# Weight slots of 16 KB: a decoder layer whose weights are laid out so that a partition's part of one load is one row of memory

## The chip, the core and the metric

The kernel runs on one NeuronCore of a Trainium2 chip. The metric is the device time of one execution in microseconds; the median of three runs is shown for the kernel before. The profile is that of one execution, taken by the hardware profiler. Its engines are PE (matmul; PEld is its weight load), DVE (vector), ACT (scalar), POOL (GpSimd) and SP (here it only issues DMAs). The data moves on 16 DMA engines.

## The reference

One post-norm decoder layer on 256 tokens of width 1024, all float32. First attention with 8 heads: with a sequence of 256 and blocks of 256 there is no earlier block to select, so it is causal softmax attention over the 256 tokens with a relative-position bias. Then a mixture of 32 experts of which each token takes 4:

```python
qkv = (x @ w_in).reshape(B, S, 3, H, Dh)
s_own = q @ k^T * scale + rel_t[:, t5_bucket(rel_own)]      # causal
t = softmax(s_own) @ v @ w_out
h = layer_norm(ALPHA * x + t, ln_g[0], ln_b[0])
logits = h @ w_router + b_router                            # top 4 of 32, softmax over the 4
for each expert e, on its tokens:
    g, u = split(h @ w_gu[e] + b_gu[e])                     # 1024 x 2048
    a = min(g, 7) * sigmoid(1.702 * min(g, 7)) * (clip(u, -7, 7) + 1)
    y += gate * (a @ w_dn[e] + b_dn[e])                     # 1024 x 1024
out = layer_norm(ALPHA * h + y, ln_g[1], ln_b[1])
```

The expert weights are 32 x (8 + 4) MB, about 403 of the 426 MB that the kernel moves, and each is read once.

## The kernel before

The program is one straight sequence per engine, in the order in which the Python code calls the instructions (`manual_schedule`); semaphores are put in for what depends on what. SP issues nearly all DMAs, in order; an issue stands on SP until its target buffer is free and until the load eight issues earlier on the same semaphore has landed, and everything behind it on SP stands with it.

*Slots.* SBUF holds 24 slots of 8 KB a partition (128 x 2048 float32, 1 MB), all from one pool, `wp`. `slot` (L89) takes one; `drop` (L98) gives some back and calls `prefetch` (L128), which fetches as many further weight chunks as there are free slots above `reserve`. Weights come through these slots in a fixed order, the list `todo`: 12 half blocks of w_in (blocks in the order 0, 2, 1, 3, 4, 5), 4 chunks of w_out, then for each expert 8 chunks of w_gu (`("gu", e, k)`, 128 rows of 2048) and 4 of w_dn (`("dn", e, j)`, 2 x 128 rows of 1024). `source` (L101) says where in DRAM a chunk stands: for w_gu a partition's part is one row of 8 KB, for w_in one row of 8 KB (the host has put it so), for w_dn and w_out two rows of 4 KB that lie 512 KB apart.

*Attention* (to about 90 us). x and the weights are split into a float32r high part and a remainder (`split`, L139: a cast on ACT into `whi`, a subtraction on DVE into `wlo`), and a product is three float32r matmuls (L283 to L285 for q and k, L309 to L311 for v, L418 to L421 for the output projection). A split takes two further slots, and gives the chunk's own back when it is done. `rel_bias` (L234) sends a table through DRAM (`rd`) and reads it back as `BT`. Small tensors have slots of their own: xh, xl, BT (later x), QT (later the gain), V, KTt, xT, then h and hT, biases, first, acts, Ys, acc.

*Router and first gather* (to 128 us): the four best experts for each token, positions in each expert's 64 slots, one-hot matrices.

*Experts* (128 to 1060 us), two at a time. `stage1` (L599) puts the bias into PSUM (L603) and then, for k = 0 to 7, waits for chunk k, does four matmuls with it (L610) and gives its slot back (`after(k)`). Then come on DVE and ACT the activation, on PE the scatter of the earlier expert (L663), the gather for the next pair (L593) and transposes (L627, L649). `stage2` (L630) does the same with the four w_dn chunks, four matmuls each (L638). After the last expert come a loop for experts with more than 64 tokens (`more_blocks`, which does not run on these inputs: only its branch shows, L714), the last scatter (L837) and the second norm.

```python
for k in range(KT):
    w = chunk(k)
    for i in range(2):
        for s in range(2):
            q = 2 * i + s
            nc.tensor.matmul(hgu[i][s * 64:(s + 1) * 64], xg(k), w[:, q * 512:(q + 1) * 512], ...)
    after(k)
```

Of the kernel before, what the change touches and what calls it, by code (L numbers as in the profile page):

```python
# [23 lines left out]
NE, TOPK = 32, 4  # L24
# [10 lines left out]
W_SLOTS = 24  # L35
CONV = 3
# [25 lines left out]
def tile_decoder_layer(ctx: ExitStack, tc, a, out):  # L62
# [49 lines left out]
    todo = [("in", b, i) for b in ORDER for i in range(2)] + [("out", 0, j) for j in range(4)]  # L112
    for e in range(NE):
        todo += [("gu", e, k) for k in range(KT)] + [("dn", e, j) for j in range(4)]
# [3 lines left out]
    def fetch(pieces=1):  # L118
        key = todo.pop()
        src = source(key)  # L120
        t = slot("w")
        k = src.shape[1]
        for i in range(pieces):
            ks = slice(i * k // pieces, (i + 1) * k // pieces)
            nc.sync.dma_start(t.rearrange("p (k c) -> p k c", k=k)[:, ks], src[:, ks])
        w_tiles[key] = t

    def prefetch():  # L128
        while todo and free_slots() > reserve[0]:
            fetch(1 if len(todo) > 1 else 2)  # L130
# [7 lines left out]

    def split(key, hi_engine, pieces=2, between=None):  # L139
        """The chunk as two float32r tiles that add up to it exactly."""  # L140
        w = take(key)
        hi, lo = slot("whi", FR), slot("wlo", FR)
        n = 2048 // pieces
# [6 lines left out]
        w_tiles["hi", key], w_tiles["lo", key] = hi, lo  # L150
        done(key)

    def done_split(key):
        done(("hi", key))
        done(("lo", key))
# [7 lines left out]
    class Stats:  # L163
        """Mean and (variance + eps)^-0.5 of rows that come in halves."""
# [14 lines left out]
        def finish(self):  # L179
            """One Newton step on the root that ScalarE gave."""  # L180
# [17 lines left out]
    xh, xl = (slot(n, FR).rearrange("p (k s) -> p k s", k=KT) for n in ("xh", "xl"))  # L198
    BT, QT, V = (slot(n) for n in ("BT", "QT", "V"))
    x, gb1, V = (t.rearrange("p (t d) -> p t d", t=2) for t in (BT, QT, V))  # L200
    BT, QT, KTt = (t.rearrange("p (h s) -> p h s", h=H) for t in (BT, QT, slot("KTt")))
# [7 lines left out]
    xT = slot("xT")  # L209
    xT3 = xT.rearrange("p (k s) -> p k s", k=KT)  # L210
    key0 = todo.pop()
    w0 = slot("w")
    w_tiles[key0] = w0
    w03 = w0.rearrange("p (k c) -> p k c", k=4)
    X_PARTS = (slice(0, 1), slice(1, 4), slice(4, 8))
    for i in range(4):
        if i < 2:
            nc.sync.dma_start(xT3[:, X_PARTS[i]], a["xT"][:, X_PARTS[i]])
        nc.sync.dma_start(w03[:, i:i + 1], source(key0)[:, i:i + 1])
    nc.sync.dma_start(xT3[:, X_PARTS[2]], a["xT"][:, X_PARTS[2]])  # L220
    fetch(2)
    nc.sync.dma_start(rb, a["rel_bias"])
    nc.sync.dma_start(oh, a["onehot"])
    for _ in range(4):
        fetch()
# [8 lines left out]
    def rel_bias():  # L234
# [4 lines left out]
        fetch()  # L239
# [26 lines left out]
    def parts(key, k):  # L266
        return tuple(take((p, key)).rearrange("p (k c) -> p k c", k=k) for p in ("hi", "lo"))
# [98 lines left out]
    for n in range(12):  # L366
# [28 lines left out]
    reserve[0] = 3  # L395
    drop(2)
# [32 lines left out]
    def norm_T(t, matmuls=None):  # L429
        """The normal rows transposed, with gain and shift on the way out of PSUM."""  # L430
# [21 lines left out]
    for j in range(2):  # L452
# [6 lines left out]
        if j == 0:  # L459
            for p in ("hi", "lo"):  # L460
                w_tiles.pop((p, ("out", 0, j)))
            used[0] -= 2
            h, hT = slot("h").rearrange("p (t d) -> p t d", t=2), slot("hT").rearrange("p (k s) -> p k s", k=KT)
# [19 lines left out]
    used[0] -= 2  # L483
    biases, first = slot("biases"), slot("first")
# [6 lines left out]
    drop()  # L491
# [11 lines left out]
    def top_experts(t):  # L503
        """The four largest logits, the lower index first where two are equal, beside four columns that are larger."""
# [6 lines left out]
    def positions(t):  # L511
        """Which of its expert's slots each choice takes: the number of earlier tokens with that expert."""
# [50 lines left out]
    drop()  # L563
# [35 lines left out]
    def stage1(xg, chunk, onehot_e, after):  # L599
# [30 lines left out]
    def stage2(aT, chunk, swap, Y, after, apart=False):  # L630
        banks = [pm.tile([128, 512], F32, name=n) for n in (("yp", "hg") if apart else ("yp",))]
        y_ps = [banks[s * apart][s * 64:(s + 1) * 64] for s in range(2)]
        for j in range(4):
            w = chunk(j).rearrange("p (k c) -> p k c", k=2)
            for k in range(2):
                kk = 2 * j + k
# [287 lines left out]
```

## Time and profile before

| | us |
|---|---|
| median of 3 runs (1080.9 to 1082.19) | 1081.65 |
| profiled execution, first to last instruction | 1077.4 |
| PE busy | 1016.4 (94%) |
| DVE busy | 239.6 (22%) |
| ACT busy | 172.3 (16%) |
| DMA, GB/s over the span | 396 |

The profiled execution gives its span alone; the median of the runs lies 4.25 us above it, for what stands ahead of the first and behind the last instruction. Times in the rows below are microseconds from the span's start. PE's matmuls are pipelined and their ends are modelled, so the starts of instructions are better read than their busy time: a matmul row that stands late behind its predecessor was waiting. TensorE's granted clock is 1.00 of full speed in nearly all of the span.

### The profile page before, as it was taken

What the parts mean: (1) busy time and instruction counts of PE and PEld (TensorE: products, weight loads), DVE (VectorE), ACT (ScalarE), POOL (GpSimd) and SP (SyncE); (2) the same over time, 40 slices, a digit from 0 to 9 for tenths busy, and PEclk for the clock granted to TensorE, in tenths of its full rate; (3) what the DMA queues carried; (4) which work ended last, traced back from release to release, by engine and by line L of the source; (5) the groups of instructions that cost most, each with busy time, mean ns of one, the idle gap of its engine ahead of it and who ended that gap; (6) DMA issues with size and microseconds to landing.
All of it is one profiled execution on the core that took longest, in us unless ns stands there. A gap on an engine that the chain in (4) does not pass through costs nothing. (4 is left out here: it accounts for less than half of the span.)

```text
span 1077.4 us, 11967 instructions
## 1 busy us (share of the span) xinstructions
PE 1016.4 (94%) x4970; PEld 443.9 (41%) x4970; DVE 239.6 (22%) x495; ACT 172.3 (16%) x316; POOL 15.4 (1%) x17
## 2 busy tenths in 40 slices
PE   9999999999999999999999999999999999999994
PEld 8988743343434343433324242323224242323331
DVE  6575602111111111111111111111101111111114
ACT  5454311011101010111101010101001010101012
POOL 0000300000000000000000000000000000000001
PEclk9999899999999999999999999999999999999998
DMA  9997799999999999999999999999999999999992
GB/s 330 411 367 272 264 375 384 419 415 418 416 418 418 419 417 417 416 416 417 416 418 418 417 418 416 417 417 417 416 417 417 418 418 417 415 415 418 418 413 88
DMA packets 78248, 426.39 MB, mean 396 GB/s; under 512 B 6793, under 2 KB 8113, under 8 KB 44113
## 3 DMA queue, kind: packets, MB, share of 16 engines
q1 hardware_dynamic: 77632, 423.52, 96.9%
q0 software_dynamic: 560, 2.10, 0.6%
q8 instruction: 40, 0.66, 0.2%
q14 instruction: 16, 0.12, 0.0%
HBM read 424.53 MB, written 1.06 MB: 395 GB/s over the span
## 5 line engine op out<-in xcount | busy, mean ns | idle before, releaser
L610 PE MATMUL hg<-w,xg 128*64 128x512 f32 x960 | 251.2, 601 | 26.3 <-DMA w<-in_w_gu 26.2
L610 PE MATMUL hu<-w,xg 128*64 128x512 f32 x960 | 246.7, 592 | 0.0
L638 PE MATMUL yp<-w,acts 128*64 128x512 f32 x1008 | 228.1, 598 | 11.2 <-ACT acts L628 11.2
L617 DVE TENSOR_SCALAR acts<-hg 128x512 f32<-128x512 f32 x32 | 22.1, 692 | 746.2 <-PE hg L610 746.2
L610 PEld LDWEIGHTS hg<-w,xg 128*64 128x64 f32 x960 | 61.0, 136 | 187.8 <-issue 102.7
L638 PEld LDWEIGHTS yp<-w,acts 128*64 128x64 f32 x1008 | 70.8, 137 | 146.2 <-issue 124.9
L610 PEld LDWEIGHTS hu<-w,xg 128*64 128x64 f32 x960 | 69.0, 137 | 137.0 <-issue 137.0
L618 ACT ACTIVATE acts<-acts 128x512 f32<-128x512 f32 x32 | 20.1, 630 | 500.2 <-DVE acts L617 500.2
L642 ACT COPY Ys<-yp 64x512 f32<-64x512 f32 x63 | 36.5, 580 | 219.2 <-PE yp L638 212.2
L593 PEld LDWEIGHTS tp<-OH,h 128*128 128x128 f32 x480 | 56.9, 192 | 8.1 <-issue 6.7
L663 PE MATMUL o<-Ys,GT 128*128 128x512 f32 x120 | 59.5, 618 | 0.0
L593 PE MATMUL tp<-OH,h 128*128 128x128 f32 x480 | 59.3, 277 | 0.0
L147 DVE TENSOR_TENSOR wlo<-w,whi 128x1024 fp32r<-128x1024 f32 (+1 forms) x36 | 38.1, 1103 | 16.3 <-ACT whi L158 16.1
L658 DVE TENSOR_TENSOR acc<-o,acc 128x512 f32<-128x512 f32 x60 | 38.4, 682 | 0.0
L663 PEld LDWEIGHTS o<-Ys,GT 128*128 128x128 f32 x120 | 20.3, 189 | 38.7 <-issue 27.3
L603 PE MATMUL hg<-biases,c 32*64 32x512 f32 x128 | 34.3, 612 | 0.0
L158 ACT CAST whi<-w 128x1024 fp32r<-128x1024 f32 (+1 forms) x36 | 32.4, 956 | 4.1 <-DMA w<-in_w_in 4.1
L603 PE MATMUL hu<-biases,c 32*64 32x512 f32 x128 | 32.7, 587 | 0.0
L283 PE MATMUL acc<-xh,whi 128*128 128x256 f32 x96 | 28.2, 294 | 0.1
L285 PE MATMUL acc<-xh,wlo 128*128 128x256 f32 x96 | 27.6, 288 | 0.2 <-DVE wlo L147 0.2
L595 ACT COPY xg<-tp 128x512 f32<-128x512 f32 x30 | 17.6, 586 | 62.5 <-PE tp L593 62.5
L284 PE MATMUL acc<-xl,whi 128*128 128x256 f32 x96 | 27.4, 286 | 0.0
(208 smaller groups left out, 670.4 us busy)
## 6 DMA issues: line engine op xcount, KB each, us to landing
w<-in_w_gu SPq DMA_DIRECT2D x256, 1024.0 KB, 19.8
w<-in_w_dn SPq DMA_DIRECT2D x127, 1024.0 KB, 20.0
w<-in_w_in SPq DMA_DIRECT2D x10, 1024.0 KB, 11.7
w<-in_w_out SPq DMA_DIRECT2D x4, 1024.0 KB, 19.0
w<-in_w_in SPq DMA_DIRECT2D x4, 256.0 KB, 5.1
w<-in_w_in SPq DMA_DIRECT2D x2, 512.0 KB, 8.5
BT<-rd SPq DMA_DIRECT2D x1, 1024.0 KB, 7.6
BT<-in_x POOLq DMA_DIRECT2D x1, 1024.0 KB, 5.3
```

What stands on the lines that cost most here:

```text
L147: nc.vector.tensor_tensor(lo[:, s], w[:, s], hi[:, s].bitcast(F32), op=OP.subtract)
L158: nc.scalar.copy(o, i)
L283: nc.tensor.matmul(o, wh[:, k, js], xh[:, kk, :], start=kk == 0, stop=False)
L284: nc.tensor.matmul(o, wh[:, k, js], xl[:, kk, :], start=False, stop=False)
L285: nc.tensor.matmul(o, wl[:, k, js], xh[:, kk, :], start=False, stop=kk == KT - 1)
L593: nc.tensor.matmul(ps[:, k * 128:(k + 1) * 128], h[:, t, kk * 128:(kk + 1) * 128], OH[:, t].rearrange("p s c -> p (s c)"), start=t == 0, s ...
L603: nc.tensor.matmul(hgu[i][s * 64:(s + 1) * 64], onehot_e, bgu[:, 2 * i + s, :], start=True, stop=False)
L610: nc.tensor.matmul(hgu[i][s * 64:(s + 1) * 64], xg(k), w[:, q * 512:(q + 1) * 512], start=False, stop=k == KT - 1)
L638: nc.tensor.matmul(y_ps[s], aT[:, kk % 4, kk // 4, :], w[:, k, HALVES[s ^ swap]], start=kk == 0, stop=kk == KT - 1)
L642: copy(Y[s * 64:(s + 1) * 64, s ^ swap, :], y_ps[s])
L658: nc.vector.tensor_tensor(d, po, d, op=OP.add)
L663: nc.tensor.matmul(po, GT[:, cb, t, :], Y[:, cb, :], start=True, stop=True)
```

## The change

A slot is now 16 KB a partition, and there are 12. The host lays the weights out so that a partition's part of one load is 16 KB in a row: w_gu as 4 chunks of 2 x 2048 columns an expert, w_dn as 2 chunks of 4 x 1024, w_out as 2, w_in one chunk for a whole block. A load is 2 MB; an expert has 6 loads instead of 12. `stage1` waits for a chunk, does the matmuls of two k with it, and then gives the slot back; `stage2` does four k for a chunk. In the attention a chunk is split half by half, the high part and the remainder in the two halves of one slot (`whl`), and the chunk's own slot comes back after its second half. Small tensors share slots by halves: xh with xl, BT with xT, QT with KTt, biases with first, acts with Ys, the second gain with its diagonals; h takes xT's place, acc takes that of x, hT that of KTt. V has a slot of which half is empty.

```diff
-W_SLOTS = 24
-CONV = 3
+W_SLOTS, SLOT = 12, 4096
+GU, DN = 4, 2
...
-        return wp.tile([128, 2048], dt, name=name, tag="w")
-
-    def free_slots():
-        return W_SLOTS - used[0]
+        return wp.tile([128, SLOT], dt, name=name, tag="w")
+
+    def halves(t):
+        return t[:, :SLOT // 2], t[:, SLOT // 2:]
...
-            return a["w_in"][e, :, k * 4:(k + 1) * 4, :]
-        if kind == "out":
-            return a["w_out"][k * 256:(k + 1) * 256, :].rearrange("(k p) c -> p k c", k=2)
-        if kind == "gu":
-            return a["w_gu"][e, k * 128:(k + 1) * 128, :].rearrange("(o p) c -> p o c", o=1)
-        return a["w_dn"][e, k * 256:(k + 1) * 256, :].rearrange("(k p) c -> p k c", k=2)
+            return a["w_in"][e]
+        return a["w_out"][k] if kind == "out" else a["w_gu" if kind == "gu" else "w_dn"][e, k]
...
-        todo += [("gu", e, k) for k in range(KT)] + [("dn", e, j) for j in range(4)]
+        todo += [("gu", e, k) for k in range(GU)] + [("dn", e, j) for j in range(DN)]
...
-            fetch(1 if len(todo) > 1 else 2)
+        while todo and W_SLOTS - used[0] > reserve[0]:
+            fetch(1 if len(todo) > 1 else 4)
...
+    def halved(key):
+
+        kind, e, i = key
+        return ((kind, e, 0), i, i) if kind == "in" else ((kind, e, i // 2), i % 2, i % 2)
...
-        w = take(key)
-        hi, lo = slot("whi", FR), slot("wlo", FR)
-        n = 2048 // pieces
+
+        whole, i, last = halved(key)
+        w = halves(take(whole).rearrange("p k c -> p (k c)"))[i]
+        hi, lo = halves(slot("whl", FR))
+        n = SLOT // 2 // pieces
...
-        w_tiles["hi", key], w_tiles["lo", key] = hi, lo
-        done(key)
+        w_tiles["hl", key] = hi, lo
+        if last:
+            done(whole)
...
-    for _ in range(4):
-        fetch()
+    for _ in range(2):
+        fetch(2)
...
         nc.sync.dma_start(rd, rrow)
-        fetch()
         nc.sync.dma_start(BT, bass.AP(tensor=rd.tensor, offset=rd.offset,
...
-        for k in range(KT):
-            w = chunk(k)
-            for i in range(2):
-                for s in range(2):
-                    q = 2 * i + s
-                    nc.tensor.matmul(hgu[i][s * 64:(s + 1) * 64], xg(k), w[:, q * 512:(q + 1) * 512],
-                                     start=False, stop=k == KT - 1)
-            after(k)
+        for j in range(GU):
+            w = chunk(j)
+            for kk in range(KT // GU):
+                k = j * (KT // GU) + kk
+                for i in range(2):
+                    for s in range(2):
+                        q = 2 * i + s
+                        nc.tensor.matmul(hgu[i][s * 64:(s + 1) * 64], xg(k), w[:, kk, q * 512:(q + 1) * 512],
+                                         start=False, stop=k == KT - 1)
+            after(j)
...
-        "w_gu": arr("moe_w_gate_up")[0],
+        "w_gu": arr("moe_w_gate_up")[0].reshape(NE, GU, KT // GU, 128, 2 * D).transpose(0, 1, 3, 2, 4),
...
-        "w_dn": arr("moe_w_down")[0],
+        "w_dn": arr("moe_w_down")[0].reshape(NE, DN, KT // DN, 128, D).transpose(0, 1, 3, 2, 4),
```

The instructions of PE, DVE, ACT and POOL stand in the same order with the same shapes in both kernels; only the names of their tiles differ. What moves is SP's list of loads. On SP at the start of the attention, around the table that goes through DRAM (rd out, BT in), there stood before:

```order
L125 DMA w<-in_w_in 128x2048 x4
L238 DMA rd<-rrow 8x383
L125 DMA w<-in_w_in 128x2048
L240 DMA BT<-rd 128x8x256
L242 DMA c<-in_consts 128x641
L243 DMA router<-in_router 128x288
L125 DMA w<-in_w_in 128x2048 x5
```

and now (BT_xT is the slot that BT shares with xT):

```order
L125 DMA w<-in_w_in 128x2048 x4
L241 DMA rd<-rrow 8x383
L242 DMA BT_xT<-rd 128x8x256
L244 DMA c<-in_consts 128x641
L245 DMA router<-in_router 128x288
L125 DMA w<-in_w_in 128x4096 x3
```

The half block that stood between rd and BT comes behind the router now, as the first half of a whole block. On SP from expert 0's w_dn to expert 2's w_gu, before:

```order
L125 DMA w<-in_w_dn 128x2x1024 x4
L125 DMA w<-in_w_gu 128x2048 x4
L486 DMA biases<-in_b_gu 32x2048
L487 DMA biases<-in_b_dn 32x1024
L125 DMA w<-in_w_gu 128x2048 x4
L125 DMA w<-in_w_dn 128x2x1024 x4
L125 DMA w<-in_w_gu 128x2048 x8
```

and now:

```order
L125 DMA w<-in_w_dn 128x4096 x2
L125 DMA w<-in_w_gu 128x4096 x2
L484 DMA biases_first<-in_b_gu 32x2048
L485 DMA biases_first<-in_b_dn 32x1024
L125 DMA w<-in_w_gu 128x4096 x2
L125 DMA w<-in_w_dn 128x4096 x2
L125 DMA w<-in_w_gu 128x4096 x4
```

The order of the data is the same, in half as many loads. On ACT the casts of blocks 2 and 1 (w_108 and w_110 are block 2, w_112 is the first half of block 1), with the semaphores that each waits for, before:

```order
L158 CAST whi_210<-w_108 128x1024 [waits DMAHW3_49]
...
L293 COPY QT_87<-acc_159 128x256 [waits DVE_49,PE_49]
...
L158 CAST whi_295<-w_110 128x1024 [waits DMAHW4_49]
...
L158 CAST whi_355<-w_112 128x1024 [waits DMAHW5_49]
...
L293 COPY KTt_89<-sc_302 128x256 [waits DVE_49,PE_49]
```

and now (w_104 is block 2, w_107 block 1):

```order
L163 CAST whl_202<-w_104 128x1024 [waits DMAHW3_49]
...
L294 COPY QT_KTt_86<-acc_151 128x256 [waits DVE_49,PE_49]
...
L163 CAST whl_274<-w_104 128x1024 [waits DMAHW4_49]
...
L163 CAST whl_333<-w_107 128x1024 [waits DMAHW5_49,DVE_49,PE_49]
...
L294 COPY QT_KTt_86<-sc_280 128x256 [waits PE_49]
```

The cast of block 1's first half now waits for PE as well: its target slot is the one that PE reads for block 2's first half.

## Rows read from the trace of the kernel before

**Rows 1.** The page: busy us of an engine; DMA busy in 40 slices, tenths

```profile
PE 1016.4 (94%) x4970; PEld 443.9 (41%) x4970; DVE 239.6 (22%) x495; ACT 172.3 (16%) x316; POOL 15.4 (1%) x17
...
DMA  9997799999999999999999999999999999999992
```

**Rows 2.** Busy time by stretch: engines in us, PE's clock, DMA share, GB/s

```profile
75.00:135.00 60.00, 57.63 (x317) 47.97 (x317) 36.47 (x94) 25.88 (x54) 12.10 (x11) 0.91 0.73 262
195.00:638.00 443.00, 430.63 (x2048) 163.20 (x2044) 72.80 (x141) 49.57 (x87) 0.00 (x0) 1.00 1.02 417
638.00:1047.00 409.00, 380.00 (x1768) 136.80 (x1768) 60.95 (x124) 43.79 (x76) 0.00 (x0) 1.00 1.02 417
```

**Rows 3.** Timeline of PE (start, us, ...), first matmuls of experts 12, 14, 24, 26, 30

```profile
464.71 1.07 PE L603 MATMUL hg<-biases,c 32*64 32x512 f32 x4
...
520.30 1.07 PE L603 MATMUL hg<-biases,c 32*64 32x512 f32 x4
...
820.28 1.07 PE L603 MATMUL hg<-biases,c 32*64 32x512 f32 x4
...
880.45 1.07 PE L603 MATMUL hg<-biases,c 32*64 32x512 f32 x4
...
1002.45 1.07 PE L603 MATMUL hg<-biases,c 32*64 32x512 f32 x4
```

**Rows 4.** Timeline of PE in expert 17, w_gu matmuls; [idle before <-releaser]

```profile
608.83 1.03 PE L610 MATMUL hg<-w,xg 128*64 128x512 f32 x4
...
610.54 1.03 PE L610 MATMUL hg<-w,xg 128*64 128x512 f32 x4
...
615.28 1.08 PE L610 MATMUL hg<-w,xg 128*64 128x512 f32 x4 [0.54 <-DMA w<-in_w_gu]
...
617.77 1.08 PE L610 MATMUL hg<-w,xg 128*64 128x512 f32 x4 [0.55 <-DMA w<-in_w_gu]
```

**Rows 5.** DMA packets from 815 to 828 us, and from 834 to 838

```profile
DMA packets 746, 5.46 MB, mean 420 GB/s; under 512 B 80, under 2 KB 80, under 8 KB 80
...
DMA packets 423, 1.64 MB, mean 410 GB/s; under 512 B 24, under 2 KB 24, under 8 KB 422
```

**Rows 6.** SP's weight loads of 181 to 184, 216 to 218, 95 to 96.5 us

```profile
L125 SPq DMA_DIRECT2D w<-in_w_gu x2: 327/328/328, 181.7 to 183.4; - x2
...
DMA to landing us min/median/max: 5.7/5.7/5.7
...
L125 SPq DMA_DIRECT2D w<-in_w_gu x1: 328/328/328, 217.0 to 217.0; - x1
...
DMA to landing us min/median/max: 12.9/12.9/12.9
...
DMA to landing us min/median/max: 4.9/4.9/4.9
```

**Rows 7.** Timeline of PE, experts 30 and 31

```profile
1017.21 1.08 PE L610 MATMUL hg<-w,xg 128*64 128x512 f32 x4 [0.54 <-DMA w<-in_w_gu]
...
1052.89 0.64 PE L638 MATMUL yp<-w,acts 128*64 128x512 f32 x1 [0.29 <-ACT acts L628]
```

**Rows 8.** The attention: timelines of SP, ACT, PE; the page's issue of BT

```profile
22.73 0.38 SPq L240 DMA_DIRECT2D BT<-rd  x1
...
BT<-rd SPq DMA_DIRECT2D x1, 1024.0 KB, 7.6
...
20.30 3.89 ACT L158 CAST whi<-w 128x1024 fp32r<-128x1024 f32 x4
...
25.47 0.28 PE L285 MATMUL ov<-xh,wlo 128*128 128x256 f32 x1
...
31.35 0.28 PE L283 MATMUL acc<-xh,whi 128*128 128x256 f32 x1
...
43.99 0.47 PE L283 MATMUL acc<-xh,whi 128*128 128x256 f32 x1
```

**Rows 9.** The page's DMA queues: packets, MB, share of 16 engines

```profile
q8 instruction: 40, 0.66, 0.2%
```

More of the change, by code (lines that the diff above doesn't have):

```diff
@@ L120, in fetch, with load @@
         src = source(key)
-        t = slot("w")
+        t = slot("w").rearrange("p (k c) -> p k c", k=src.shape[1])
+        load(t, src, pieces)
+        w_tiles[key] = t
+    def load(t, src, pieces):
         k = src.shape[1]
@@ L124, in fetch @@
             ks = slice(i * k // pieces, (i + 1) * k // pieces)
-            nc.sync.dma_start(t.rearrange("p (k c) -> p k c", k=k)[:, ks], src[:, ks])
-        w_tiles[key] = t
+            nc.sync.dma_start(t[:, ks], src[:, ks])
     def prefetch():
-        while todo and free_slots() > reserve[0]:
-            fetch(1 if len(todo) > 1 else 2)
+        while todo and W_SLOTS - used[0] > reserve[0]:
+            fetch(1 if len(todo) > 1 else 4)
     def take(key):
@@ L149, in split @@
                 between(i)
-        w_tiles["hi", key], w_tiles["lo", key] = hi, lo
-        done(key)
+        w_tiles["hl", key] = hi, lo
+        if last:
+            done(whole)
     def done_split(key):
-        done(("hi", key))
-        done(("lo", key))
+        done(("hl", key))
     def act_copy(o, i):
@@ L196, in tile_decoder_layer @@
     p1 = hctx.enter_context(tc.tile_pool(name="p1", bufs=1, space=PSUM))
[L198 to L201, printed above, removed]
+    xh, xl = (t.rearrange("p (k s) -> p k s", k=KT) for t in halves(slot("xhl", FR)))
+    (BT, xT), (QT, KTt), (V, _) = (halves(slot(n)) for n in ("BT_xT", "QT_KTt", "V"))
+    x, acc, h, gb1, V = (t.rearrange("p (t d) -> p t d", t=2) for t in (BT, BT, xT, QT, V))
+    hT = KTt.rearrange("p (k s) -> p k s", k=KT)
+    BT, QT, KTt = (t.rearrange("p (h s) -> p h s", h=H) for t in (BT, QT, KTt))
     rb = hp.tile([32, H], F32, name="rb")
@@ L266, in parts @@
     def parts(key, k):
-        return tuple(take((p, key)).rearrange("p (k c) -> p k c", k=k) for p in ("hi", "lo"))
+        return tuple(t.rearrange("p (k c) -> p k c", k=k) for t in take(("hl", key)))
     open_ps = {}
@@ L459, in tile_decoder_layer @@
         if j == 0:
[L460 to L463, printed above, removed]
+            w_tiles.pop(("hl", ("out", 0, j)))
+            used[0] -= 1
         else:
@@ L482, in tile_decoder_layer @@
     out_part(3, 1, (2,))
-    used[0] -= 2
-    biases, first = slot("biases"), slot("first")
+    used[0] -= 1
+    biases, first = halves(slot("biases_first"))
     bgu, bdn, gT = biases[:NE], biases[NE:2 * NE, :D], biases[NE:2 * NE, D:D + S]
@@ L632, in stage2 @@
         y_ps = [banks[s * apart][s * 64:(s + 1) * 64] for s in range(2)]
[L633 to L636, printed above, removed]
+        for j in range(DN):
+            w = chunk(j)
+            for k in range(KT // DN):
+                kk = j * (KT // DN) + k
                 for s in range(2):
@@ L704, in more_blocks @@
     def more_blocks():
-        bufs = itertools.cycle([slot("lw") for _ in range(4)])
-        spare = slot("spare")
+        bufs = itertools.cycle([slot("lw") for _ in range(2)])
+        spare = first
         Y2 = spare[:, :1024].rearrange("p (b c) -> p b c", b=2)
@@ L747, in more_blocks, with chunk, gu_chunk @@
             quarter(1)
-            def load(key_src, k):
-                t = next(bufs)
-                nc.sync.dma_start(t.rearrange("p (k c) -> p k c", k=k), key_src)
-                return t
-            def gu_chunk(k):
-                return load(a["w_gu"][bass.ds(e_reg, 1), k * 128:(k + 1) * 128, :].rearrange("o p c -> p o c"), 1)
+            def chunk(name, i):
+                src = a[name][bass.ds(e_reg, 1), i].rearrange("o p k c -> p (o k) c")
+                t = next(bufs).rearrange("p (k c) -> p k c", k=src.shape[1])
+                nc.sync.dma_start(t, src)
+                return t
+            def gu_chunk(j):
+                return chunk("w_gu", j)
             def dn_chunk(j):
-                return load(a["w_dn"][bass.ds(e_reg, 1), j * 256:(j + 1) * 256, :]
-                            .rearrange("o (k p) c -> p (o k) c", k=2), 2)
+                return chunk("w_dn", j)
             hgu = stage1(lambda k: xg[:, k, :CAP], gu_chunk, sel_e.to_broadcast([NE, CAP]), lambda k: None)
@@ L775, in tile_decoder_layer @@
     Gd = pair_gates(0, OH)
-    GT = Y = acc = None
-    reserve[0] = 3
+    GT = Y = None
+    reserve[0] = 1
     for p in range(NE // 2):
@@ L789, in tile_decoder_layer @@
             if e == 0:
-                acts = slot("acts")
+                acts, Ys = halves(slot("acts_Ys"))
                 act3 = [acts[:, i * 512:(i + 1) * 512] for i in range(3)]
                 aT = acts[:, 1536:].rearrange("p (j s c) -> p j s c", j=4, s=2)
-                Ys = slot("Ys").rearrange("p (i b c) -> p i b c", i=2, b=2)
-                reserve[0] = 1
-            elif e == 1:
-                acc = slot("acc").rearrange("p (t d) -> p t d", t=2)
+                Ys = Ys.rearrange("p (i b c) -> p i b c", i=2, b=2)
                 reserve[0] = 0
@@ L820, in tile_decoder_layer @@
             if e == NE - 2:
-                gb2, diagonals = slot("gb2"), slot("diagonals")
+                gb2, diagonals = halves(slot("gb2_diag"))
                 for kk in range(2 * KT):
@@ L831, in tile_decoder_layer @@
     sm = [mp.tile([128, 8], F32, name=f"sm{t}") for t in range(2)]
-    sq = slot("sq")[:, :D]
+    sq = diagonals[:, :D]
     def mean_neg(t):
```

24 lines of the change are left out of this document (8 added, 16 removed).

## The prediction

> **What bounds the kernel now.** Read first the page's busy lines and slices: PE is busy 94% of the span and the DMA row reads 9 almost throughout [rows 1], so the average does not say which of the two ends last. The table by stretch does [rows 2]: from 195 us on the DMA share is 1.02 at 417 GB/s, while PE's busy time falls from 431 of 443 us before 638 us to 380 of 409 us after it. The starts of experts two apart say the same [rows 3]: the pair from 464.71 to 520.30 took 55.59 us (PE's own pace), the pair from 820.28 to 880.45 took 60.17. Between them PE's work did not grow; it waits. The timeline shows for what [rows 4]: its w_gu matmuls start 1.72 us apart while weights are in stock (608.83 to 610.54) and then 2.49 us apart, each behind a landing (615.28, 617.77). So two stages have two limits: up to expert 15 PE works off weights loaded ahead, from expert 16 on the end is set by the weight stream alone. The stream never stands still after 195 us, so what counts is the time of one load, and where the stream stands when it last had to wait for a slot.
>
> **The change, part by part.** PE, DVE, ACT and POOL keep their instructions and order; SP's loads change.
>
> *Time of a load.* A stretch in which only w_gu moves has 746 packets for 5.46 MB, all but 80 tiny ones of 8 KB, at 420 GB/s; one with only w_dn has 422 of 423 packets under 8 KB (4 KB rows, 256 a load) at 410 GB/s [rows 5]. So 1024 KB takes 2.49 us in 128 packets (also PE's spacing in [rows 4]) and 1.0486 MB / 410 GB/s = 2.56 us in 256. The 128 packets more cost 0.07 us; the bytes alone then take 2.42. A 2048 KB load with 128 rows of 16 KB, if a row is one packet, takes 2 x 2.42 + 0.07 = 4.91 us, against 4.98 for two w_gu loads and 5.12 for two w_dn loads. No weight row of 16 KB is in this trace. Bounds: 4.84 (packets cost nothing), 4.98 (16 KB no better than 8 KB). I take 4.91, the straight line through both measured sizes. Per expert: 4 x 0.07 + 2 x 0.21 = 0.70 us less, 30.16 before and 29.46 after; a pair 58.9, still above PE's 55.59, so the stream stays the bound.
>
> The Trainium skill has a rule that would make this smaller: "DMA: Bandwidth & Descriptors", section "Why small descriptors are slow", gives a fixed overhead of about 3 cycles a packet, 3.5 ns at the 850 MHz of its section "Specifications". Measured here are 0.07 us for 128 packets on 16 engines, 8 a piece, so about 8.8 ns. An expert goes from 128 to 48 packets per engine; 80 x 3.5 ns is an estimate of 0.28 us by that page, and the whole would come to 1078.5 us instead of the sum below. The measured price decides.
>
> *Where the stream stands.* Slots come back as 16 KB now, when both halves have been read, and the early stretch is where slots limit: DMA share 0.73 from 75 to 135 us [rows 2]. I follow SP's order with PE's times of before. The last load that finds the stream empty is expert 3's second w_gu load: it takes the slot of expert 1's first w_dn load, whose second half PE has read at 183.4 (there stand two issues now, at 181.7 and 183.4, one for each half [rows 6]). A load on an idle stream lands 4.9 us after its issue [rows 6], 2.5 of them its own bytes, so 2.4 us pass first. From that load to expert 4's last w_gu load there are nine: 183.4 + 2.4 + 9 x 4.91 = 230.0. Before, expert 4's last load was issued at 217.0 and landed 12.9 us later, at 229.9 [rows 6]. So at 230 us both stand at the same load. But before, landings from 187.4 (181.7 + 5.7) to 229.9 took 42.5 us for 12 w_gu and 4 w_dn loads, whose sum is 40.1; the 2.4 us over that, which I can't place, I let the changed kernel pay too. Cost +2.4 (bounds 0 and +5).
>
> *Sum over the stream.* The last time PE waits for weights is expert 30's last w_gu load, at 1017.2 [rows 7]; after it expert 30's extra transposes (L700) and the last expert run at PE's pace, and what PE waits for there is ACT (1052.89) [rows 7]. From expert 4's last w_gu load to expert 30's are 26 experts: 26 x 0.70 = 18.2 us less.
>
> *Tail.* That landing now brings two rows of k at once: PE has 3.43 us of matmuls behind it instead of 1.72. Cost +1.72. Expert 31's w_dn loads land 34 to 39 us after that point (29.46 for its w_gu, then 4.91 each) and are wanted from 1052.89 - 1017.21 + 1.72 = 37.4 us on [rows 7], one k every 0.9 us, so they add nothing.
>
> *At nothing.* The w_in load between rd and the bias table BT is gone, so BT comes earlier and the following blocks come whole instead of in halves. Block 3 can land at the latest 7.6 us after BT's issue at 22.73 plus c, router and its own 4.91, about 37 us; its two casts (1 us each) and a subtraction end near 40, and PE wants it at 43.99 [rows 8]. The cast of block 1's first half now waits for PE's end of block 2's first half, about 25.7 instead of 22.2; two casts and a subtraction are done near 29.6, and PE starts on it at 31.35 [rows 8]. Behind it on ACT stand two PSUM copies that wait for that same PE work anyway. If this cover of 1.7 us were gone, every later release would shift by the overshoot, one for one. Each later block comes 4.9 us behind the one before, while PE takes 12.6 for one (31.35 to 43.99). In the expert stage the narrowest is expert 3's second w_gu load: it lands at 190.7, when PE has nearly all of expert 2 still in front of it (a pair takes 55.59, an expert 28). The merged small tensors and the loop over spare blocks, which does not run here, cost nothing.
>
> Sum: -18.2 + 2.4 + 1.7 = -14.1 us. The profiled execution has a span of 1077.4 us; the median of the runs is 1081.65, 4.25 above, which I carry over. Span 1063.3, median **1067.5 us**.
>
> **Rivals.**
> *16 KB rows are no better than 8 KB rows* (a row is cut in two, or the cost goes with bytes from there). Then only w_dn gains: 26 x 4 x 0.07 = 7.3, and -7.3 + 2.4 + 1.7 = -3.2, 1078.5 us. For it: no weight packet above 8 KB is in the trace. Against: the instruction queue moves 0.66 MB in 40 packets, 16 KB each [rows 9], and 4 KB and 8 KB rows each go as one packet [rows 5]. The time that the page's 3 cycles gave is nearly this one's.
>
> *Coarse slots starve the stream: slower.* Place: the 19 loads between 75 and 183 us, when SP waits for PE to hand back slots. Price: if each stands still for the reading of its second half, 1.72 us, with nothing queued in front, that is 32.7 us: -18.2 + 32.7 + 1.7 = +16.2, 1097.9 us. It decides from 16.5 us of extra standing on. For it: DMA idles a quarter of 75 to 135 us already [rows 2]. Against: in the order followed above most of these loads queue behind one still moving, and 4.91 us a load catches up before 230. "Perfetto Trace Analysis" of the Trainium skill, section "DMA Optimizations", names this side: when the engines are generally idle, smaller pieces may start sooner. Here they are idle only before 195 us.
>
> *The stream stops being the bound.* Then expert 30 starts at PE's pace, 520.30 + 8 x 55.59 = 965.0 instead of 1002.45 [rows 3], and the time is 37.4 less, 1044.2. It needs 1024 KB in 2.32 us, below the 2.42 that the bytes alone take.
>
> **How the numbers follow.** Chances: the forecast 0.80, no gain above 8 KB 0.13, starved stream 0.05, PE's pace 0.02. The forecast's own range runs from 4.84 us a load with the early 2.4 us paid (26 x 1.12 = 29.1 less, -25.0, 1056.6) to half the row gain with +5 early (-12.7 + 5 + 1.7 = -6, 1075.7). To leave out no more than 2 in 10 I reach to the second case: 1058 to 1079. About 0.2%, 2.2 us, is what a measurement can tell from no change. Faster: 0.78 of the first, 0.08 of the second, 0.02 of the last, 0.88; the same 0.06; slower 0.06.
>
> **What would show it.** Right: 128 packets per 2048 KB load, GB/s near 427 in stretches of the expert stage, pairs of experts 58.9 us apart after about expert 18, the first wait of PE for w_gu some two experts later than now, 3.4 us of w_gu matmuls behind each such wait, expert 4's last w_gu load landing between 229 and 235. Wrong: rows cut into 8 KB packets, GB/s at 420; a DMA share well below 1 after 195 us; waits of PE for weights in experts 0 to 4; new waits for casts in the attention.

## The result and the profile after

The changed kernel takes **1064.22 us** (median of 4 runs, 1062.38 to 1065.89) against 1081.28 (4 runs) for the kernel before: 17.1 us less by the medians; the ratio, which is that of the means, is 0.9845 (95% interval 0.9824 to 0.9865), 16.8 us less. Forecast were 1067.5, between 1058 and 1079.

The page of the changed kernel, busy lines and DMA packets (answering [rows 1]), the packets of the kernel before, which moved the same bytes, and those of the changed kernel from 500 to 520 us:

```profile
PE 1010.5 (95%) x4970; PEld 447.6 (42%) x4970; DVE 239.2 (22%) x495; ACT 172.4 (16%) x316; POOL 15.3 (1%) x17
...
DMA packets 33396, 426.36 MB, mean 401 GB/s; under 512 B 3672, under 2 KB 4992, under 8 KB 7712
...
DMA packets 78248, 426.39 MB, mean 396 GB/s; under 512 B 6793, under 2 KB 8113, under 8 KB 44113
...
DMA packets 584, 8.52 MB, mean 426 GB/s; under 512 B 64, under 2 KB 64, under 8 KB 64
```

In the last line all but 64 tiny packets carry 16 KB each (520 x 16 KB are the 8.52 MB): a weight row goes as one packet, and a load of 2048 KB is 128 of them.

Its table by stretch, with the columns of [rows 2]:

```profile
75.00:135.00 60.00, 57.65 (x317) 48.00 (x317) 36.68 (x95) 25.84 (x54) 12.09 (x11) 0.91 0.79 287
195.00:638.00 443.00, 434.18 (x2074) 165.70 (x2072) 72.75 (x141) 50.67 (x89) 0.00 (x0) 1.00 1.01 428
638.00:1030.00 392.00, 367.39 (x1736) 136.39 (x1734) 60.81 (x124) 42.58 (x74) 0.00 (x0) 1.00 1.01 427
```

The stream is still what ends last from 195 us on, now at 428 GB/s instead of 417. PE's timeline, answering [rows 3] and [rows 4]: the first wait for w_gu (in expert 17), two waits in expert 19, the first matmuls of experts 24 and 26, the last two waits (expert 29), the first matmul of expert 30, the one with which expert 30's last load is first used, and the last scatter:

```profile
615.80 1.08 PE L608 MATMUL hg<-w,xg 128*64 128x512 f32 x4 [0.91 <-DMA w<-in_w_gu]
...
671.10 1.08 PE L608 MATMUL hg<-w,xg 128*64 128x512 f32 x4 [1.24 <-DMA w<-in_w_gu]
...
676.00 1.08 PE L608 MATMUL hg<-w,xg 128*64 128x512 f32 x4 [1.24 <-DMA w<-in_w_gu]
...
810.49 1.07 PE L599 MATMUL hg<-biases_first,c 32*64 32x512 f32 x4
...
869.27 1.07 PE L599 MATMUL hg<-biases_first,c 32*64 32x512 f32 x4
...
966.27 1.08 PE L608 MATMUL hg<-w,xg 128*64 128x512 f32 x4 [1.23 <-DMA w<-in_w_gu]
...
971.17 1.08 PE L608 MATMUL hg<-w,xg 128*64 128x512 f32 x4 [1.25 <-DMA w<-in_w_gu]
...
988.20 1.07 PE L599 MATMUL hg<-biases_first,c 32*64 32x512 f32 x4
...
1000.53 1.08 PE L608 MATMUL hg<-w,xg 128*64 128x512 f32 x4
...
1046.96 5.40 PE L831 MATMUL o<-acts_Ys,GT 128*128 128x512 f32 x8 [1.94 <-issue]
```

A wait is followed by the next one 4.90 us later, and a pair of experts takes 58.78. The first wait of the kernel before and its last scatter, for comparison (its first wait falls in expert 15, two experts earlier):

```profile
557.56 1.08 PE L610 MATMUL hg<-w,xg 128*64 128x512 f32 x4 [0.20 <-DMA w<-in_w_gu]
...
1061.89 3.90 PE L837 MATMUL o<-Ys,GT 128*128 128x512 f32 x8 [1.91 <-DVEq L714]
```
SP's issues of expert 3's second w_gu load, expert 4's last and expert 30's last, with the time to landing (answering [rows 6]):

```profile
L125 SPq DMA_DIRECT2D w<-in_w_gu x1: 328/328/328, 183.7 to 183.7; - x1
...
DMA to landing us min/median/max: 8.1/8.1/8.1
...
L125 SPq DMA_DIRECT2D w<-in_w_gu x1: 328/328/328, 218.9 to 218.9; - x1
...
DMA to landing us min/median/max: 13.4/13.4/13.4
...
L125 SPq DMA_DIRECT2D w<-in_w_gu x1: 328/328/328, 961.6 to 961.6; - x1
...
DMA to landing us min/median/max: 38.9/38.9/38.9
```

With the second and the third of these issues the two profiled executions (1077.4 and 1063.9) can be laid side by side:

| us | before | after | difference | forecast |
|---|---|---|---|---|
| to expert 4's last w_gu landing | 229.9 | 232.35 | +2.4 | +2.4 |
| from there to expert 30's last w_gu landing | 787.3 | 768.1 | -19.2 | -18.2 |
| from there to the end | 60.2 | 63.4 | +3.2 | +1.7 |
| span | 1077.4 | 1063.9 | -13.5 | -14.1 |

(Expert 30's last load: issued at 961.6, landed at 1000.49; before, PE's start at 1017.21 [rows 7] stands for it.) The medians differ by 17.1, more than the profiles' 13.5. The time of the changed kernel's profiled execution is 1065.89, 2.0 above its span, and if that holds for both, the profile of the kernel before caught a quick execution (1079.4), and that of the changed kernel the slowest of four: 2.2 us of the 4.25 that the prediction carried over are this.

### The profile page after: what moved, and what is told of

It is laid out like the page before. It is cut to its first block, busy times and chain, and to the rows that moved or that the text cites. A ratio compares the mean times of both kernels' runs of the same rounds, so it can differ in the third digit from the quotient of the medians.

```text
span 1063.9 us, 11574 instructions
## 1 busy us (share of the span) xinstructions
PE 1010.5 (95%) x4970; PEld 447.6 (42%) x4970; DVE 239.2 (22%) x495; ACT 172.4 (16%) x316; POOL 15.3 (1%) x17
## 5 line engine op out<-in xcount | busy, mean ns | idle before, releaser
L636 PE MATMUL yp<-w,acts_Ys 128*64 128x512 f32 x1008 | 228.0, 598 | 11.2 <-ACT acts_Ys L626 11.2
L636 PEld LDWEIGHTS yp<-w,acts_Ys 128*64 128x64 f32 x1008 | 70.8, 137 | 146.1 <-issue 128.9
L640 ACT COPY acts_Ys<-yp 64x512 f32<-64x512 f32 x63 | 36.5, 579 | 219.2 <-PE yp L636 212.1
L589 PEld LDWEIGHTS tp<-OH,BT_xT 128*128 128x128 f32 x480 | 56.9, 192 | 8.1 <-issue 6.7
L661 PE MATMUL o<-acts_Ys,GT 128*128 128x512 f32 x120 | 59.5, 618 | 0.0
L589 PE MATMUL tp<-OH,BT_xT 128*128 128x128 f32 x480 | 59.3, 277 | 0.0
L152 DVE TENSOR_TENSOR whl<-w,whl 128x1024 fp32r<-128x1024 f32 (+1 forms) x36 | 38.2, 1103 | 21.6 <-ACT whl L163 21.6
L656 DVE TENSOR_TENSOR BT_xT<-o,BT_xT 128x512 f32<-128x512 f32 x60 | 38.4, 681 | 0.0
L599 PE MATMUL hg<-biases_first,c 32*64 32x512 f32 x128 | 34.3, 612 | 0.0
L599 PE MATMUL hu<-biases_first,c 32*64 32x512 f32 x128 | 32.7, 587 | 0.0
L284 PE MATMUL acc<-xhl,whl 128*128 128x256 f32 x96 | 28.4, 296 | 0.4 <-ACT whl L163 0.4
L286 PE MATMUL acc<-xhl,whl 128*128 128x256 f32 x96 | 27.7, 289 | 0.2 <-DVE whl L152 0.2
L285 PE MATMUL acc<-xhl,whl 128*128 128x256 f32 x96 | 27.5, 287 | 0.0
```

Source lines behind the costliest of these rows:

```text
L152: nc.vector.tensor_tensor(lo[:, s], w[:, s], hi[:, s].bitcast(F32), op=OP.subtract)
L284: nc.tensor.matmul(o, wh[:, k, js], xh[:, kk, :], start=kk == 0, stop=False)
L285: nc.tensor.matmul(o, wh[:, k, js], xl[:, kk, :], start=False, stop=False)
L286: nc.tensor.matmul(o, wl[:, k, js], xh[:, kk, :], start=False, stop=kk == KT - 1)
L589: nc.tensor.matmul(ps[:, k * 128:(k + 1) * 128], h[:, t, kk * 128:(kk + 1) * 128], OH[:, t].rearrange("p s c -> p (s c)"), start=t == 0, s ...
L599: nc.tensor.matmul(hgu[i][s * 64:(s + 1) * 64], onehot_e, bgu[:, 2 * i + s, :], start=True, stop=False)
```

## The experiments

P is the theory that a packet has a price, 0.07 us for 128 packets on 16 engines, and nothing else in the change gains. Its rival L says that larger and fewer loads gain.

**The rows alone, the slots alone.** Three kernels keep the changed one's slots and loads and lay weights out in other rows; a fourth keeps the slots of the kernel before. The lines show where a load's source is named; the host's layouts, which change with it, are left out.

```diff
 r1_gu_8k (r4_gu_2k: rows of 512 columns, k=8)
-            return a["w_gu"][e, k]
+            return a["w_gu"][e, k].rearrange("k p c -> p k c")       # rows of 8 KB
 r2_old_rows: the same for w_gu, w_dn and w_out                        # 8, 4 and 4 KB
 b1_dn_8k (kernel before)
-        return a["w_dn"][e, k * 256:(k + 1) * 256, :].rearrange("(k p) c -> p k c", k=2)
+        return a["w_dn"][e, k]                                        # laid out by the host, 8 KB
```

> The changed kernel with its slots, loads and DMA count; only the 2048 KB loads of w_gu are laid out in rows of 8 KB (256 packets a load instead of 128). Theory P (the gain is a price per packet, 0.07 us per 128 packets on 16 engines): landings of w_gu 4.96 to 4.97 us apart instead of 4.89, 4 x 0.07 = 0.28 us more an expert, 26 experts: +7.3 us, about 1071.5. Rival L (the gain comes from fewer and larger loads, not from their rows): landings stay at 4.89, 1064.2. Rival with rows of 16 KB no better than 8 KB: 1064.2 as well, and then the gain would have to be w_dn's alone.

> The slots and the 2048 KB loads alone: all weight rows as they were before the change (w_gu 8 KB, w_dn and w_out 4 KB), in 12 slots of 16 KB. Theory P: per expert 4 x 0.07 + 2 x 0.21 = 0.70 us more than the changed kernel, 26 experts: +18.2, about 1082.4; worked from the kernel before it is 1081.3 + 2.4 (early slots) + 1.7 (tail) = 1085.4. So 1082 to 1086, not below the kernel before. Rival L (fewer and larger loads): about 1064 to 1068.

> The changed kernel with w_gu in rows of 2 KB: 1024 packets in a 2048 KB load instead of 128. Theory P as a straight line: 4.89 + 7 x 0.07 = 5.38 us a load, 1.96 us more an expert, 26 experts: +51, about 1115. A price of 3 cycles a packet (3.5 ns, as the Trainium skill's page DMA: Bandwidth & Descriptors has it, 0.028 us per 128 packets): 5.09 us a load, +20, about 1084.6. If small rows cost more than the straight line: above 1118.

> The kernel before with 24 slots of 8 KB; only w_dn is laid out so that a partition's part of a load is one row of 8 KB (128 packets in 1024 KB instead of 256). Theory P: w_dn lands 2.49 us apart instead of 2.55 to 2.56, 4 x 0.065 = 0.26 us an expert, 26 experts: -6.8 us, ratio to the kernel before 0.9937, with no cost in the early slots or the tail. Rival L (load size is what counts): ratio 1.000.

Measured: r1_gu_8k 1074.54 us, ratio to the kernel before 0.9943 (0.9923 to 0.9963); r2_old_rows 1083.92, 1.0037 (1.0018 to 1.0057); r4_gu_2k 1124.92, 1.0415 (1.0395 to 1.0436); b1_dn_8k 1071.28, 0.9916 (0.9900 to 0.9933). The waits of PE for w_gu, one behind the other, in r1_gu_8k and then in r4_gu_2k:

```profile
856.17 1.08 PE L610 MATMUL hg<-w,xg 128*64 128x512 f32 x4 [1.31 <-DMA w<-in_w_gu]
...
861.12 1.08 PE L610 MATMUL hg<-w,xg 128*64 128x512 f32 x4 [1.30 <-DMA w<-in_w_gu]
```

```profile
832.74 1.08 PE L610 MATMUL hg<-w,xg 128*64 128x512 f32 x4 [1.76 <-DMA w<-in_w_gu]
...
838.14 1.08 PE L610 MATMUL hg<-w,xg 128*64 128x512 f32 x4 [1.75 <-DMA w<-in_w_gu]
```

and the stretch from 638 us of r2_old_rows, which is back at the 417 GB/s of [rows 2]:

```profile
638.00:1030.00 392.00, 359.23 (x1691) 132.88 (x1688) 60.80 (x124) 41.41 (x72) 0.00 (x0) 1.00 1.02 417
```

The landings of 2048 KB loads between 235 and 980 us stand apart by these medians (the last column counts the pairs of successive landings that the trace holds):

| row | packets | us | kernel, pairs |
|---|---|---|---|
| 16 KB | 128 | 4.89 | the changed kernel, all loads, 113 |
| 8 KB | 256 | 4.97 | r1_gu_8k, w_gu, 75 |
| 4 KB | 512 | 5.11 | r2_old_rows, w_dn, 37 |
| 2 KB | 1024 | 5.41 | r4_gu_2k, w_gu, 69 |

A straight line: 0.072 to 0.075 us per 128 packets from 16 KB rows down to 2 KB, and 4.82 us for the bytes. From expert 4's to expert 30's last w_gu landing r1_gu_8k takes 775.7 us, r2_old_rows 787.0 and r4_gu_2k 821.9, that is 7.6, 18.8 and 53.8 more than the changed kernel (expected 7.3, 18.2, 51). What their times have beyond that lies mostly before expert 4, whose last load lands 2.8 us later in r1_gu_8k (where expert 0 began 1.2 us later and the clock fell further, see below) and 5.3 in r4_gu_2k (where the early loads are slower too). The time of r4_gu_2k lies above the 1118 from which its expectation would have small rows dearer than the straight line; the load's own 5.41 us, against 5.38 expected, says that they are not. P holds. L falls: with large loads and the old rows r2_old_rows takes 787.0 us for this stretch, and the kernel before took 787.3. As a whole it is 4.1 us slower than the kernel before, which is what slots (+2.4) and tail (+1.7) were put at. And b1_dn_8k gains with the old loads; its w_dn lands 2.485 apart instead of 2.55, and the 9 us of its runs are more than the 6.8 expected, by 0.4 at the nearest end of the interval.

**Twice as many DMAs.** Each load in two DMAs of 64 partitions, in two ways:

```diff
-            nc.sync.dma_start(t[:, ks], src[:, ks])
+            for ps in (slice(0, 64), slice(64, 128)):                  # r3_two_dmas
+            for ps in (slice(0, 128, 2), slice(1, 128, 2)):            # r5_even_odd
+                nc.sync.dma_start(t[ps, ks], src[ps, ks])
```

> The changed kernel with each weight load issued as two DMAs of 64 partitions each: twice as many DMAs and completions, the same 16 KB packets and the same number of them. Theory P: pairs of DMAs land 4.89 us apart as now, 1064.2 within 2 us. Rival L (what was saved is a cost per DMA, 0.70 us an expert over six loads): most of the gain is lost, about 1078 to 1082.

> As the run with two DMAs a load, but one DMA takes the even and one the odd partitions instead of the lower and the upper 64. Theory W (what was slow there is that all 16 engines write into the same half of the partitions at a time; each packet of 16 KB took about twice as long): packets take 0.6 us as in the changed kernel, about 1064, within 3 us. Rival (a DMA of 64 rows, or twice as many DMAs, is slow by itself): about 1450 to 1600 again. Theory P with a cost per DMA that the earlier runs could not see: between, 1066 to 1080.

Measured: r3_two_dmas 1542.33 us (1453 to 1624), r5_even_odd 1068.86, ratio 0.9903 (0.9882 to 0.9924). Neither theory had the first, and even its quickest execution is a third slower than the kernel before; its trace is that of the slowest. Packets from 600 to 640 us in r3_two_dmas, and its two stretches, then those of r5_even_odd:

```profile
DMA packets 717, 9.40 MB, mean 235 GB/s; under 512 B 143, under 2 KB 143, under 8 KB 143
...
195.00:638.00 443.00, 316.85 (x1159) 111.93 (x1155) 41.08 (x79) 28.29 (x50) 0.00 (x0) 0.83 1.01 227
638.00:1030.00 392.00, 310.60 (x1312) 114.39 (x1310) 44.84 (x85) 31.59 (x55) 0.00 (x0) 0.92 1.01 336
```

```profile
195.00:638.00 443.00, 432.70 (x2064) 165.24 (x2062) 72.79 (x141) 50.67 (x89) 0.00 (x0) 1.00 1.01 428
638.00:1030.00 392.00, 368.65 (x1742) 140.78 (x1740) 60.94 (x124) 42.58 (x74) 0.00 (x0) 1.00 1.01 427
```

The engines are busy all the time in both (share 1.01), but in r3_two_dmas a 16 KB packet takes about 1.1 us (16 x 40 us for some 574 of them) instead of 0.6. With even and odd partitions nothing is lost in the stretches, and two DMAs land 2.45 apart each. So it is not the number of DMAs but which 64 rows one of them takes. These are partitions of SBUF on one side and rows of DRAM on the other, and no run changes one alone; but 64 adjacent rows of 16 KB are 1 MB of DRAM in one piece, and so is a w_gu load of the kernel before, which takes 2.49 us over 128 partitions. That speaks for the partitions. The Trainium skill's page "SBUF — State Buffer", section "Door 1: The DMA port swizzle", says so: the lower 64 partitions reach 8 of the 16 ports that DMAs write through, and the upper 64 the other 8, for some 218 GB/s. The 227 GB/s come near that; that where the rate is 336 the two halves' packets ran beside each other is a guess that no row shows. Of the 1.3 us that r5_even_odd's profile has over the changed kernel's, 1.1 stand ahead of expert 4's last w_gu landing; the 4.6 of its runs I can't place.

**Where a microsecond counts.** Twelve matmuls with unused results, ahead of expert 0 or of expert 8:

```diff
+            if e == 0:                                                 # 8 in d8_delay_e8
+                ps = tp_tile()
+                for i in range(12):
+                    nc.tensor.matmul(ps, ones, h[:, 0, :512], start=i == 0, stop=i == 11)
```

> The changed kernel with twelve idle matmuls (128 x 128 by 512 columns, results unused) on PE ahead of expert 0's weights, at about 129 us: some 5.2 us of PE time at the 0.43 us that the scatter's matmuls stand apart. Theory: before 184 us the stream waits for slots that PE gives back, so PE's delay shifts the stream and the end one for one: about 1069.4, expert 4's last w_gu load lands near 237.5 instead of 232.35. Rival (the stock of loaded weights hides it, as anywhere else in the PE-paced stage): 1064.2.

> The same twelve matmuls ahead of expert 8, at about 354 us, where PE is still paced by itself but SP's issues stand some 20 us ahead of their landings. Theory (from 195 us on only the stream counts): nothing at the end, 1064.2 within 1 us; the first wait of PE for w_gu comes later than expert 17. Rival (PE's work in its own paced stage adds to the end): 1069.4.

Measured: d0_delay_e0 1075.98 us, ratio 0.9957 (0.9943 to 0.9971); d8_delay_e8 1064.45, 0.9853 (0.9836 to 0.9869). PE's timeline of d0_delay_e0, the matmuls and the starts of experts 0 and 30, and its landing of expert 4's last w_gu load; then the same of d8_delay_e8 around expert 8, with its first wait for weights:

```profile
128.93 10.57 PE L785 MATMUL tp<-BT_xT,ones 128*128 128x512 f32 x24
139.42 1.07 PE L599 MATMUL hg<-biases_first,c 32*64 32x512 f32 x4
...
998.68 1.07 PE L599 MATMUL hg<-biases_first,c 32*64 32x512 f32 x4
...
L125 SPq DMA_DIRECT2D w<-in_w_gu x1: 327/327/327, 229.6 to 229.6; - x1
...
DMA to landing us min/median/max: 13.4/13.4/13.4
```

```profile
354.44 10.57 PE L785 MATMUL tp<-BT_xT,ones 128*128 128x512 f32 x24
...
794.14 1.08 PE L608 MATMUL hg<-w,xg 128*64 128x512 f32 x4 [1.23 <-DMA w<-in_w_gu]
...
988.90 1.07 PE L599 MATMUL hg<-biases_first,c 32*64 32x512 f32 x4
```

I had counted half: a float32 matmul stands as two instructions, and twelve took 10.5 us. Ahead of expert 0 they shift expert 4's landing by 10.6 (229.6 + 13.4 = 243.0), expert 30's start by 10.5 (988.20 to 998.68) and the median by 11.8. The same 10.5 us ahead of expert 8 shift the start of expert 30 by 0.7, of which 0.6 were there at expert 0, and the median by 0.2; PE only meets the stream later, at 794 instead of 616. The theory holds in both places: up to the last slot that the stream waits for, PE's time is the kernel's time; in expert 8 PE had these 10.5 us to spare.

**The tail and the work ahead of the last slot.** Four kernels try to use this: halves for the last loads, and two pieces of PE's work moved.

```diff
 t1_tail
-            fetch(1 if len(todo) > 1 else 4)
+            fetch(4 if len(todo) == 1 else 2 if todo[-1] in LATE else 1)   # w_gu's last load, experts 29 to 31
 m1_move (left out: the gather's second quarter; the first scatter, which now writes acc)
-            look_ahead = ahead_pair and s == (p > 0)
+            look_ahead = ahead_pair and s == 1
-            elif e == 1:
+            if e == 9:
                 start_acc()
 best: both.  best2: t1_tail and start_acc in expert 9, with this in expert 1:
+                    nc.tensor.matmul(ps, ones, h[:, 0, :512], start=i == 0, stop=i == 2)   # three times
```

> The changed kernel with the last w_gu load of experts 29, 30 and 31 in two DMAs of one k each (8 KB rows, 2.48 us each): in the trace of the changed kernel PE waits last for weights at 971.17 us, for expert 29's last w_gu load, and runs 3.43 us of matmuls behind it; expert 30's last load, at 1000.49, comes 0.07 us before it is wanted. Theory: with halves PE has one k, 1.72 us, behind expert 29's last landing, and what gives out next are expert 30's third load (landing 995.59, wanted at 995.3 by then): 1.3 to 1.5 us less, about 1062.8. Rival (the tail's 1.7 us was never paid, since expert 30 does not wait): 1064.2.

> The changed kernel with two pieces of PE's work moved behind the last slot that the stream waits for: the gather of the second pair stands in expert 1 instead of expert 0, and the start of acc (eight matmuls of 32 rows, in whose wake the granted clock was 0.73 from 178 to 184 us) in expert 9 instead of expert 1; the first scatter writes acc instead of adding to it. Theory: expert 0's first w_dn slot comes back at about 151.7 instead of 153.2 and expert 1's at about 180 instead of 183.7, so the stream gains 2.1 us by expert 4's last w_gu load (230.2 instead of 232.35) and keeps it: about 1062.1. In expert 9 the moved work and its lower clock cost nothing. Rival (moved work comes back at the end one for one): 1064.2 or more.

> Both of these together, the last w_gu loads of experts 29 to 31 in halves and the two pieces of PE's work moved. Theory: the gains add, -1.4 - 2.1: about 1060.7. If the loads at the end only follow the stream, the sum is smaller: 1062.

> The changed kernel with the last w_gu loads of experts 29 to 31 in halves, the start of acc in expert 9 instead of expert 1, three idle matmuls (2.6 us, results unused) in its place in expert 1 so that PE does not stand idle there, and the second pair's gather back in expert 0. Theory: expert 0 takes 27.77 us again and the clock stays at 1.00 from 172 to 184 us; expert 1's first w_dn slot comes back about 50.9 us after expert 0's start instead of 54.9, and the stream then waits only for its own earlier loads: expert 4's last w_gu load lands 103.0 us after expert 0's start (103.6 in the changed kernel's profile, 104.6 in a run where the clock fell further), and 1.4 us less behind expert 29: about 1062, ratio to the kernel before 0.983. Rival (the clock falls elsewhere in its place, or expert 1 is not what the stream waits for): 103.6 or more, 1064.

Measured: t1_tail 1065.33 us, ratio 0.9855 (0.9835 to 0.9875); m1_move 1065.58, 0.9862 (0.9845 to 0.9879); best 1065.12, 0.9861 (0.9845 to 0.9878); best2 1063.27, 0.9841 (0.9828 to 0.9855). By time none can be told from the changed kernel's 0.9845, so a version that is shown to be faster did not come of it. The first three lie above 1064.2, the time without any gain; best2 lies between that and the 1062 of its theory. The traces say what happened.

In t1_tail expert 30 starts 1.6 us earlier against its own landings (its last w_gu load landed at 1002.84 and PE starts the expert at 988.94, where the changed kernel has 1000.49 and 988.20). The gain is there, and is covered by where the stream stood: 2.3 us later at expert 4. Of these, 1.2 are expert 0's start (130.01 instead of 128.79). For the rest its table shows the cause, in the two stretches around expert 1's second half (PE's clock is the third column from the end):

```profile
988.94 1.07 PE L600 MATMUL hg<-biases_first,c 32*64 32x512 f32 x4
...
172.00:178.00 6.00, 5.51 (x18) 2.01 (x15) 4.05 (x6) 0.99 (x2) 0.00 (x0) 0.90 1.00 429
178.00:184.00 6.00, 6.00 (x17) 2.57 (x17) 2.27 (x6) 1.17 (x2) 0.00 (x0) 0.53 1.00 429
```

In the second stretch the granted clock is at half speed (1.2 of 2.4 GHz) nearly throughout; in the changed kernel that stretch has 0.73, in the kernel before 0.74, and in r4_gu_2k 1.00. Where it falls, it falls in or just behind `start_acc`, four matmuls (eight instructions) that use 32 rows of the array, and what it costs stands ahead of the last slot: expert 1 took 32.1 us in t1_tail, 30.4 in the changed kernel and 29.2 in r4_gu_2k.

m1_move takes that work away and loses the clock in another place. PE's timeline of expert 0, and its clock there:

```profile
148.82 0.63 PE L625 MATMUL tp<-c,acts_Ys 128*128 128x128 f32 x4 [3.00 <-DVE acts_Ys L619]
150.12 8.62 PE L636 MATMUL yp<-w,acts_Ys 128*64 128x512 f32 x32 [0.68 <-ACT acts_Ys L626]
...
150.00:155.00 5.00, 4.88 (x16) 1.57 (x18) 0.00 (x0) 0.07 (x1) 0.00 (x0) 0.67 0.40 170
```

Without the gather PE stands idle for 3.0 us while the activation runs, the clock falls behind it, and the w_dn matmuls take 8.6 us instead of 7.1. In best, with the same edit, the clock of this stretch is 0.50 and they take 9.5; in every other profile of these experiments but r3_two_dmas, where the gather stands in its place, it is 1.00. The gather had covered that gap. best2 leaves it there and fills expert 1's gap:

```profile
173.18 2.84 PE L805 MATMUL tp<-BT_xT,ones 128*128 128x512 f32 x6
...
177.19 7.09 PE L637 MATMUL yp<-w,acts_Ys 128*64 128x512 f32 x32 [0.29 <-ACT acts_Ys L627]
...
178.00:184.00 6.00, 6.00 (x30) 1.87 (x26) 0.00 (x0) 0.00 (x0) 0.00 (x0) 1.00 1.00 426
...
1044.84 3.90 PE L840 MATMUL o<-acts_Ys,GT 128*128 128x512 f32 x8 [1.98 <-issue]
```

The clock stays at 1.00, expert 4's last w_gu load lands 101.95 us after expert 0's start (103.6 in the changed kernel, 103.0 expected), and PE reaches the last scatter at 1044.84 instead of 1046.96, with an expert 0 that began 0.9 us later. That is about 3 us in the trace; the runs show 1 us with intervals that overlap.

## Why the prediction was right, point by point

*Time of a load.* 4.91 forecast, 4.89 measured, between the bounds 4.84 and 4.98; the three kernels with other rows put three more points on the same line. The rival with 16 KB rows no better than 8 KB falls by r1_gu_8k: 0.075 us a load, 7.6 us over 26 experts. The straight line also tells against the price of 3 cycles a packet in the Trainium skill's "DMA: Bandwidth & Descriptors", section "Why small descriptors are slow": 0.0735 us for 128 packets, 8 an engine, is 9.2 ns each, not the 3.5 that the prediction worked out from it.

*26 experts.* 18.2 forecast, 19.2 measured. An expert takes 29.54 us, of which six loads are 29.37; before it was 30.28 against a forecast of 30.16. What lies over the loads comes in six landings that are 0.7 to 0.9 late, 4.6 us between 235 and 990; in the kernel before three landings that are 1.5 late make the same 4.6, so that the difference is the time of a load alone.

*Where the stream stands.* The landing at 232.35 hit the forecast 232.4, and the load named as the last that finds the stream empty is that: issued at 183.66, landed 8.1 later, 5.48 behind the one before. That the sum was met is in part luck. The load landed at 191.77 instead of the forecast 190.7, and two landings behind it, at 197.57 and 227.46, are 0.9 and 0.7 late: less 0.3 for loads quicker than 4.91, these are the 2.4 us that the forecast carried over without placing them. And its cause is sharper than I had it. It is not slots as such but PE's time before that release, one for one (d0_delay_e0), and part of that time is a fallen clock in or behind `start_acc`, in both kernels. From execution to execution this moves: expert 0 starts between 128.3 and 130.0 over the profiles with the changed slots and no delay ahead of it (r3_two_dmas left out), and expert 1 takes 29.2 to 32.1 us in those that keep its work as it was.

*Tail.* Here a step failed, though its size did not: "the last time PE waits for weights is expert 30's last w_gu load". It is expert 29's, at 971.17; expert 30's last load then lands as PE comes to it, with no wait (the row at 1000.53). From that landing to the end r1_gu_8k, r2_old_rows and d0_delay_e0, whose last scatter takes 3.90 us as before, need 62.0 us instead of 60.2, so the two rows of k cost 1.8, against the 1.72 forecast; with halves t1_tail needs 60.7. The rest of the +3.2 is the last scatter: 5.40 us in this execution and 3.90 before (the rows at 1046.96 and 1061.89 above), at a granted clock of 0.70 from 1046.9 to 1052.5. Of thirteen profiles (all but r3_two_dmas) seven show 3.90 and six 5.40 to 5.60; what decides that stays open. So the profiles' -13.5 came near the forecast -14.1 in part by luck: the 1.0 us more that the loads gave and the scatter's 1.5 stand against each other.

*At nothing.* Expert 0 starts at 128.79, before at 128.57, so the blocks that come whole cost next to nothing. The cast that now waits for PE stood 3.5 us, and PE waited 0.6 us in all for casts and subtractions:

```profile
ACT whl L163 <- PE ov L286: 3.5, 1, 3.5
```

*Rivals.* Starved stream: r2_old_rows prices slots and tail together at +4.1 us, not at the +34.4 (32.7 and 1.7) of this rival. PE's pace: the stream still ends last, and with 4.82 us for the bytes of a load it must.

## What to carry to other kernels

When a stream of loads is the bound, find the last load that had to wait for a buffer: here everything ahead of it on PE, the engine that gives that buffer back, counted one for one. Behind it what counted was the time of a load and, after the last wait for weights, the tail; 10.5 us of added work on PE between them cost nothing. Price a layout by rows: a price per packet, measured from two row sizes in the trace, gave the load time of a third within 0.02 us of 4.89. Work that looks movable may be covering a gap; look at what the engine does, and at its clock, in the place it leaves.

## What the runs showed of the hardware

- A row of 16 KB goes as one packet (520 of them for 8.52 MB), and the price per packet is the same from 2 KB to 16 KB rows: 0.072 to 0.075 us for 128, so 9.2 ns on its engine.
- Loads in DMAs of the lower and the upper 64 partitions moved 227 GB/s in one stretch and 336 in the next (r3_two_dmas), in DMAs of even and odd partitions 428 and 427 (r5_even_odd).
- The granted clock fell to half in or behind four matmuls of 32 rows (0.53 from 178 to 184 us in t1_tail) and behind 3.0 us of idle time (0.50 from 150 to 155 us in best). The first cost 1.3 to 2.9 us of expert 1, measured from r4_gu_2k, whose clock did not fall; the second 1.5 and 2.4 us of the w_dn matmuls.
- A packet of instructions may delay the load beside it. From 191.8 to 197.6 us in the changed kernel the queues for instructions moved a packet of 16 KB and one of 8 KB:

```profile
DMA packets 166, 2.45 MB, mean 422 GB/s; under 512 B 16, under 2 KB 16, under 8 KB 16
...
q8 instruction: 1, 0.02, 1.0%
q14 instruction: 1, 0.01, 0.3%
```

and the load of this stretch landed 5.80 us behind its predecessor instead of 4.89. Beside the landing at 227.46 (5.55) there is a packet of 16 KB too. But most such packets delay nothing: from 235 to 990 us there are 27, each of the six late landings has one beside it, and 21 go without. That a packet causes a late landing is read from this coincidence, not tested, and what sets the six apart stays open.
